# First stage in a written order: filter products one or two tiles ahead, scale's last half between them

## The chip, the cores and the metric

The kernel runs on one core of a Trainium2 chip. The metric is the device time of one execution in microseconds (us). The engines are TensorE (PE; its weight loads are shown apart as PEld), VectorE (DVE), ScalarE (ACT), GpSimd (POOL), and SyncE (SP), which here only issues DMAs. PSUM is the memory that TensorE writes; a bank holds 128 x 512 fp32.

## The reference, cut to what matters

The model is three blocks in a row on an input of 512 tokens by 1024 channels: attention with dilations beside a gated recurrence, then a block with latent attention and a long convolution, then a hybrid block. The change lies in what is done before the first projection. Four pieces of it are computed there.

```
# block 1: modulated norm of the input
mod = silu(c) @ w_ada + b_ada;  shift, scale, gate = split(mod, 3)
h = rmsnorm(x, norm_g) * (1 + scale) + shift
q_a, k_a, v_a, ... = split(h @ w_in)
# block 1: table of relative biases for the attention (rel_bias, by bucket of distance)
# block 2, wanted much later: filters of the long convolution and an embedding
h = sin(fr * (z @ w1 + b1)); h = sin(fr * (h @ w2 + b2)); h = sin(fr * (h @ w3 + b3))
h = (h @ w_out).reshape(L, 2, 512) * decay       # forward and backward filter
kf = rfft(concat(h_fwd, 0, reversed h_bwd))      # spectrum of the filter
e = p @ w_ple                                    # per-layer embedding
```

## The kernel before, in words

All activations are held transposed: 8 tiles of 128 channels by 512 tokens. A product is made nearly exact in fp32 by splitting each operand into a high part (rounded, written by ACT) and a low part (the rest, a subtraction on DVE or POOL), and by three matmuls, high with high, low with high and high with low (`acc_T`). `parts` splits a weight tile of 128 x 1024, `split` an activation, into the tiles `wh` and `wl`, or a high and a low tile. Weights are loaded by SP into four raw buffers (`wr`) that are handed out in turn; there are three pairs of `wh` and `wl`.

The order of instructions on each engine is set by a planner, which keeps the order of the data and takes, at each moment of its own clock, the work that is ready, what was written earlier first. Where the kernel opens a region with `manual_schedule`, the instructions of the named engines keep the order in which they are written; how the engines stand against each other, and where work from outside the region falls between, stays with the planner. Before the change only TensorE's order in the recurrence of block 1 is written so. Each engine's queue is worked off in order: an instruction that waits holds everything behind it.

The stage is the function `start`. Its parts:

- `early.load0`, `load1`, `load_fw`: the loads for the work that block 2 needs (positions `c_z`, filter layers `fw`, embedding input `pt`, its weights `w2ple`, filter output weights `fwo`, decays `dec`, transform matrices `c_fw`).
- `early.layer(i)`: a product of 64 by 64 for both halves of the positions, a reduction of the angle on DVE (seven operations), and a sine on ACT; three in a row.
- `early.emb`: eight products of the embedding with 6 matmuls each, copied out of PSUM by ACT into the tiles A, which hold the normed input later, and stored to memory (`scr_e`).
- squares of the input x on ACT, their sum on DVE, `col_sums` (TensorE), `rsqrt` (a DVE operation and a power on POOL), `rows` (TensorE spreads the result over the partitions, ACT copies it to `bc`).
- `early.filt(t)`, for four tiles of time: two filter products into banks `s`, two products with the decay on DVE, their sum on POOL and difference on DVE, and the splits of both: `sm` with the low part on DVE, `df` with it on POOL.
- `AdaRows`, for scale and for shift: eight tiles `adar` of 512 KB, six buffers for both; four thin matmuls per tile (32 columns of weights, 256 elements moved), accumulated in the one bank `o`; then `columns`: a copy on ACT, two transposes, an addition on DVE.
- DVE multiplies each x tile with the gain and `bc`; with shift, ACT writes the high part of the tile A, DVE its low part. This is `h`.
- `early.spectrum(f)`, for two halves of the frequencies: 24 matmuls on `sm` and `df` (`halves`), ACT copies, POOL's difference and sum, stores to `scr_kf` that are issued from ACT's queue.
- `rel_table`: two products, copies to a tile, a store, from which the attention's loads are made.

Of the second spectrum and of the table, TensorE's part is put behind the transposes of shift (`issue_after`). The first projection, `attn1`, starts with the product of `w1q` with `h` in `proj_T`.

## Time and profile before

| | us |
|---|---|
| median of the timed runs (3; 2255.76 to 2261.93) | 2259.17 |
| the profiled execution: its own time | 2263.86 |
| its span | 2262.1 |
| TensorE busy in the span (97%) | 2193.2 |
| DVE busy (61%) | 1372.2 |
| ACT busy (42%) | 947.0 |
| POOL busy (23%) | 529.1 |
| first matmul of q's projection starts at | 84.75 |

The span is that of one profiled execution. A line of the profile names the line of the kernel, the engine, the operation, what it writes and what it reads; x is the count, and in brackets or behind a bar stands the idle time of the engine before it, with what ended it. A line of a helper (L116 is the matmul) stands for many places, so the names of the tiles tell which one is meant: `pa` is the embedding, `fwo` a filter product, `adar` a tile of scale or shift, `sm` and `df` the spectrum, `A` the normed input. An fp32 matmul appears as two instructions. The granted clock is TensorE's, as a share of full speed.

### The profile page before, as it was taken

What the parts mean: (1) busy time and instruction counts of PE and PEld (TensorE: products, weight loads), DVE (VectorE), ACT (ScalarE), POOL (GpSimd) and SP (SyncE); (2) the same over time, 40 slices, a digit from 0 to 9 for tenths busy, and PEclk for the clock granted to TensorE, in tenths of its full rate; (3) what the DMA queues carried; (4) which work ended last, traced back from release to release, by engine and by line L of the source; (5) the groups of instructions that cost most, each with busy time, mean ns of one, the idle gap of its engine ahead of it and who ended that gap; (6) DMA issues with size and microseconds to landing.
All of it is one profiled execution on the core that took longest, in us unless ns stands there. A gap on an engine that the chain in (4) does not pass through costs nothing.

```text
span 2262.1 us, 30194 instructions
## 1 busy us (share of the span) xinstructions
PE 2193.2 (97%) x11672; PEld 1793.4 (79%) x11672; DVE 1372.2 (61%) x2226; ACT 947.0 (42%) x1597; POOL 529.1 (23%) x454
## 2 busy tenths in 40 slices
PE   7898999999999998999999999999999999999998
PEld 4677788888888976688888886798888788888886
DVE  6564777753354598478647647877666754433333
ACT  4344556642243456544324434455544233222221
POOL 3233555521122225221001103000111221310220
PEclk7899999999999999999999999999999999999999
DMA  8552122224323342233232243222222422223322
GB/s 317 183 162 75 54 94 85 84 75 130 103 88 110 115 136 75 68 109 101 79 110 102 70 153 118 87 83 75 80 95 83 140 84 94 94 83 112 98 79 76
DMA packets 80728, 235.27 MB, mean 104 GB/s; under 512 B 9887, under 2 KB 10911, under 8 KB 80584
## 3 DMA queue, kind: packets, MB, share of 16 engines
q1 hardware_dynamic: 65768, 208.25, 28.2%
q10 hardware_dynamic: 14816, 25.08, 3.4%
q8 instruction: 92, 1.51, 0.3%
q14 instruction: 52, 0.43, 0.1%
HBM read 218.60 MB, written 15.22 MB: 103 GB/s over the span
## 4 chain that ended last, share of the span: by engine, by line
PE 56%; DVE 2%; issue 2%; ACT 1%; POOL 0%; POOLq 0%; DVEq 0%; ACTq 0%
PE mm L116 49%; PE s L116 3%; PE o L116 2%; PE t L116 1%; DVE sg L1772 0%; PE t L1612 0%; ACT wh L110 0%; DVE x L2438 0%; DVE st L1597 0%; DVE wl L111 0%; DVE x L1773 0%; DVE B L212 0%; PE t L2123 0%; ACT A L211 0%; PE t L2086 0%
## 5 line engine op out<-in xcount | busy, mean ns | idle before, releaser
L116 PE MATMUL mm<-A,wh 128*128 128x512 f32 x2176 | 691.1, 393 | 1.0 <-DVE A L212 1.0
L110 ACT CAST wh<-wr 128x1024 fp32r<-128x1024 f32 (+2 forms) x374 | 368.4, 987 | 609.6 <-PE mm L116 398.5
L111 DVE TENSOR_TENSOR wl<-wr,wh 128x1024 fp32r<-128x1024 f32 (+3 forms) x371 | 446.2, 1204 | 275.4 <-ACT wh L110 274.3
L116 PE MATMUL mm<-B,wh 128*128 128x512 f32 x1672 | 536.2, 396 | 1.3 <-DVE us L268 0.9
L116 PEld LDWEIGHTS mm<-A,wh 128*128 128x128 f32 x2176 | 409.6, 189 | 89.3 <-issue 1.9
L116 PE MATMUL mm<-A,wl 128*128 128x512 f32 x1088 | 425.8, 392 | 4.3 <-DVE wl L111 4.3
L116 PEld LDWEIGHTS mm<-B,wh 128*128 128x128 f32 x1672 | 313.5, 188 | 72.7 <-issue 4.0
L116 PE MATMUL mm<-B,wl 128*128 128x512 f32 x836 | 329.2, 394 | 0.0
L116 PEld LDWEIGHTS mm<-A,wl 128*128 128x128 f32 x1088 | 205.4, 189 | 47.7 <-DVE wl L111 6.3
L116 PEld LDWEIGHTS mm<-B,wl 128*128 128x128 f32 x836 | 157.3, 188 | 35.0 <-issue 3.0
L251 POOL TENSOR_TENSOR r<-r,mhalf 128x4 f32<-128x4 f32 (+1 forms) x40 | 53.2, 1332 | 407.6 <-DVE r L250 407.6
L116 PE MATMUL mm<-a,wh 128*128 128x512 f32 x448 | 140.5, 389 | 0.0
L268 DVE TENSOR_TENSOR us<-mm,bc 128x512 f32<-128x512 f32 x95 | 65.1, 688 | 97.2 <-PE mm L116 95.8
L204 POOL TENSOR_TENSOR a<-sl,a 128x512 fp32r<-128x512 f32 x28 | 40.5, 1446 | 274.2 <-ACT a L202 274.2
L116 PEld LDWEIGHTS mm<-a,wh 128*128 128x128 f32 x448 | 84.1, 188 | 17.5
L116 PE MATMUL mm<-a,wl 128*128 128x512 f32 x224 | 86.8, 389 | 0.0
L116 PE MATMUL mm<-wh,A 128*128 128x256 f32 x448 | 84.8, 285 | 0.0
L116 PEld LDWEIGHTS mm<-wh,A 128*128 128x128 f32 x448 | 71.0, 191 | 1.2 <-issue 0.6
L2358 POOL TENSOR_TENSOR sl<-sl,bc 128x512 f32<-128x512 f32 x22 | 28.7, 1305 | 167.6 <-DVE sl L1718 167.6
L116 PE MATMUL mm<-wl,A 128*128 128x256 f32 x224 | 63.6, 284 | 0.0
L116 PE MATMUL mm<-wh,B 128*128 128x256 f32 x320 | 61.2, 287 | 0.0
L1747 DVE TENSOR_TENSOR x<-x,mm 128x512 f32<-128x512 f32 x32 | 22.0, 687 | 64.5 <-PE mm L116 64.5
(588 smaller groups left out, 3472.0 us busy)
## 6 DMA issues: line engine op xcount, KB each, us to landing
wr<-w2upg SPq DMA_DIRECT2D x22, 512.0 KB, 3.4
wr<-w2upu SPq DMA_DIRECT2D x22, 512.0 KB, 3.4
wr<-w3fg SPq DMA_DIRECT2D x22, 512.0 KB, 3.4
wr<-w3fu SPq DMA_DIRECT2D x22, 512.0 KB, 3.4
adar<-w1ada SPq DMA_DIRECT2D x16, 512.0 KB, 7.6
wr<-w3out SPq DMA_DIRECT2D x16, 512.0 KB, 3.5
wr<-w1ib SPq DMA_DIRECT2D x14, 512.0 KB, 3.5
wr<-w2uh SPq DMA_DIRECT2D x12, 512.0 KB, 3.4
```

The lines of the kernel that those rows point to most:

```text
L110: nc.scalar.copy(out=hi[:, :n], in_=r[:, :n])
L111: (eng or nc.vector).tensor_tensor(out=lo[:, :n], in0=r[:, :n], in1=hi[:, :n].bitcast(F32), op=ALU.subtract)
L116: return self.nc.tensor.matmul(out, a, b, start=start, stop=stop)
L204: eng.tensor_tensor(out=l[:p], in0=src, in1=hi[:p].bitcast(F32), op=ALU.subtract)
L251: nc.gpsimd.tensor_tensor(out=r, in0=r, in1=self.mhalf[:, :n], op=ALU.pow)
L268: self.nc.vector.tensor_tensor(out=out, in0=ps, in1=bc, op=ALU.mult)
L1747: k.nc.vector.tensor_tensor(out=xs[n], in0=xs[n], in1=ps, op=ALU.add)
L2358: nc.gpsimd.tensor_tensor(out=s, in0=s, in1=norm.bc, op=ALU.mult)
```

## The change

All five engines' instructions in `start` now keep the written order, and that order is new.

- The loads: embedding inputs and weights alternate; the table's inputs come before x; then scale's first four tiles, filter output weights, decays, and shift's first four tiles. Scale has four buffers of its own; shift goes into the two tiles of each A(i), as halves of 256 KB. Scale's last four tiles, shift's others and the transform matrices follow. The embedding is held in eight tiles of its own and stored after all these loads; the spectrum's copies later use the same tiles.
- The embedding is issued in pairs, between the layers and scale's first half. Scale's first half comes before the filter, its second half after the rows of the norm, between the filter products.
- Filter products are issued one or two tiles before the work on their results, into banks `s` and `mm` by turns. Sum and difference are both on DVE, both low parts on POOL.
- The first transform matrix is split by POOL, the second by DVE. The spectrum is issued in four halves, one before shift's last tiles, one among the normed inputs, two at the end; its sums come last (the sum on DVE, the difference on POOL), and its stores go through SP.
- The load and the split of the first `w1q` tile are written in `start`, before the last two halves' products.

```diff
@@ proj_T
-            self.acc_T(ps, self.w(s, nk * P, eng), act, nk, i == 0, i == len(nks) - 1, k0=k0)
+            w, self.first = self.first or self.w(s, nk * P, eng), None
+            self.acc_T(ps, w, act, nk, i == 0, i == len(nks) - 1, k0=k0)
@@ AdaRows
-    def load(self):
+    def load(self, kks, places=None):
...
+        for kk in kks:
+            src = k.aps["w1ada"][self.part, kk]
+            if places:
+                r = places[kk]
+                for j in range(2):
+                    k.nc.sync.dma_start(out=r[j], in_=src[:, j * T : (j + 1) * T])
+            else:
+                t = self.pool.tile([P, D], F32, tag="adar", bufs=4, name=k.name("adar"))
+                k.nc.sync.dma_start(out=t, in_=src)
...
+    def step(self, n):
         k = self.k
-        ps = k.bank("o", 1)
-        for kk, r in enumerate(self.r):
+        if self.n == 0:
+            self.ps = k.bank(*(("mm", 3) if self.part == 0 else ("o", 1)))
+        for kk in range(self.n, self.n + n):
...
@@ start
-    with k.tc.tile_pool(name="b1s", bufs=1) as pool:
+    with k.tc.tile_pool(name="b1s", bufs=1) as pool, k.tc.manual_schedule(
+        engines={E.PE, E.Activation, E.DVE, E.Pool, E.SP}
+    ):
+        scale, shift = AdaRows(k, pool, 1), AdaRows(k, pool, 0)
         early.load0(pool)
+        rb, oh = rel_load(k, pool)
...
+        scale.load(range(4))
         early.load1()
...
+        places = [[t.bitcast(F32) for t in k.A(i)] for i in range(NK)]
+        shift.load(range(4), places)
...
+        early.layer(0)
+        early.parts(0)
+        early.sin()
+        early.parts(1)
+        early.emb(2)
+        early.layer(1)
+        early.emb(2)
+        early.sin()
+        early.layer(2)
+        square(2)
+        scale.step(2)
+        early.emb(2)
+        square(2)
+        early.sin()
+        scale.step(2)
+        scale.load(range(4, 8))
+        shift.load(range(4, 6), places)
+        early.load_fw(0)
+        shift.load(range(6, 8), places)
+        early.load_fw(1)
+        early.emb(2)
+        early.filt_ps(0)
+        square(4)
+        early.filt_ps(1)
+        sums = k.col_sums(acc)
+        early.filt(0)
+        r = k.rsqrt(sums, NT, 1.0 / D)
+        early.filt_ps(2)
+        shift.step(2)
+        bc = k.rows(r)
+        early.filt(1)
+        scale.step(4)
+        early.filt_ps(3)
+        early.store()
+        early.filt(2)
+        shift.step(2)
         sc1 = scale.columns()
+        early.fparts(0)
+        early.filt(3)
         (the gain of each x tile, then its product with the gain and bc, as before)
+        early.halves(0, 0)
+        shift.step(4)
         sh = shift.columns()
+        early.fparts(1)
+        tab = rel_table(k, rb, oh)
         (for each i: the high and the low part of A(i), as before)
+            if i == 4:
+                early.halves(0, 1)
+        k.first = k.w(k.aps["w1q"][0])
+        early.halves(1, 0)
+        early.halves(1, 1)
+        early.sums()
@@ Early2.filt_ps, filt
+            ps = k.bank(*(("mm", 3) if t % 2 else ("s", 2)))
+            k.mm(ps, self.cur[r, t % 2 * P : t % 2 * P + P], self.wo[r, j * 512 : (j + 1) * 512], True, True)
...
-            (nc.gpsimd if add else nc.vector).tensor_tensor(out=s, in0=fb[0], in1=fb[1], op=op)
-            l.append(k.split(k.pair(p, f"{nm}{t}"), s, lo="v" if add else "g"))
+            nc.vector.tensor_tensor(out=s, in0=fb[0], in1=fb[1], op=op)
+            l.append(k.split(k.pair(p, f"{nm}{t}"), s, lo="g"))
@@ Early2.fparts, halves, sums
+        self.fw_parts.append(self.k.parts(self.cw[f], eng=None if f else self.k.nc.gpsimd))
...
+                t = self.p.tile([P, T], F32, tag=f"e{4 * f + 2 * j + i}", name=k.name("ab"))
+                nc.scalar.copy(out=t, in_=ps)
...
             nc.gpsimd.tensor_tensor(out=d, in0=a, in1=b, op=ALU.subtract)
-            nc.gpsimd.tensor_tensor(out=a, in0=a, in1=b, op=ALU.add)
+            nc.vector.tensor_tensor(out=a, in0=a, in1=b, op=ALU.add)
             for i, s in enumerate((a, d)):
-                nc.scalar.dma_start(out=self.kf[j, 2 * f + i], in_=s)
+                nc.sync.dma_start(out=self.kf[j, 2 * f + i], in_=s)
```

More of the change, by code (lines that the diff above doesn't have):

```diff
@@ L495, in start @@
             xs.append(x)
+        scale.load(range(4))
         early.load1()
-        early.load_fw(0)
-        early.load_fw(1)
-        scale, shift = AdaRows(k, pool, 1), AdaRows(k, pool, 0)
-        scale.load()
+        places = [[t.bitcast(F32) for t in k.A(i)] for i in range(NK)]
+        shift.load(range(4), places)
         c = k.v("c", 0, 8)
@@ L506, in start, with square @@
         nc.vector.tensor_scalar(out=sc, in0=sc, scalar1=0.5, scalar2=None, op0=ALU.mult)
-        for i in range(3):
-            early.layer(i)
-        early.emb(range(NK))
         acc = k.nm.tile([P, T], F32, tag="sqa", bufs=1, name=k.name("xa"))
-        for i in range(NK):
-            q = pool.tile([P, T], F32, tag="xq", bufs=3, name=k.name("xq")) if i else acc
-            nc.scalar.activation(out=q, in_=xs[i], func=AF.Square)
-            if i:
-                nc.vector.tensor_tensor(out=acc, in0=acc, in1=q, op=ALU.add)
-        bc = k.rows(k.rsqrt(k.col_sums(acc), NT, 1.0 / D))
-        for t in range(NT):
-            early.filt(t)
-        shift.load()
+        qs = []
+        def square(n):
+            for i in range(len(qs), len(qs) + n):
+                q = pool.tile([P, T], F32, tag="xq", bufs=3, name=k.name("xq")) if i else acc
+                nc.scalar.activation(out=q, in_=xs[i], func=AF.Square)
+                qs.append(q)
+                if i:
+                    nc.vector.tensor_tensor(out=acc, in0=acc, in1=q, op=ALU.add)
+        early.layer(0)
[34 more added lines that the diff above has]
+        shift.step(2)
         sc1 = scale.columns()
+        early.fparts(0)
+        early.filt(3)
         ga = k.cp.tile([P, NK], F32, tag="gada", name="gada")
         nc.vector.scalar_tensor_tensor(out=ga, in0=sc1, scalar=1.0, in1=k.v("norm_g", 0, 8), op0=ALU.add, op1=ALU.mult)
-        early.spectrum(0)
         for i in range(NK):
@@ L537, in start @@
             h.append((hi, lo))
-        with k.tc.issue_after(mark):
-            early.spectrum(1)
-            tab = rel_table(k, pool)
+            if i == 4:
[4 more added lines that the diff above has]
+        early.sums()
     return h, tab
@@ L1221, in emb, with store, filt_ps @@
             k.acc_T(ps, (hi[:, o:], lo[:, o:]), self.pa, 2)
-            e = k.A(n)[0].bitcast(F32)
+            e = p.tile([P, T], F32, tag=f"e{n}", name=f"e{n}")
             nc.scalar.copy(out=e, in_=ps)
-            nc.sync.dma_start(out=self.ed[n], in_=e)
+            self.es.append(e)
+    def store(self):
+        for n, e in enumerate(self.es):
+            self.k.nc.sync.dma_start(out=self.ed[n], in_=e)
+    def filt_ps(self, t):
+        k = self.k
+        r = slice(t // 2 * 64, t // 2 * 64 + 64)
+        self.fps[t] = []
+        for j in range(2):
+            ps = k.bank(*(("mm", 3) if t % 2 else ("s", 2)))
+            k.mm(ps, self.cur[r, t % 2 * P : t % 2 * P + P], self.wo[r, j * 512 : (j + 1) * 512], True, True)
+            self.fps[t].append(ps)
+    fps = {}
     def filt(self, t):
@@ L1228, in filt @@
         fb = []
-        for j in range(2):
-            ps = k.bank("s", 2)
-            r = slice(t // 2 * 64, t // 2 * 64 + 64)
-            k.mm(ps, self.cur[r, t % 2 * P : t % 2 * P + P], self.wo[r, j * 512 : (j + 1) * 512], True, True)
+        for ps in self.fps[t]:
             f = self.tmp()
```

69 lines of the change are left out of this document (42 added, 27 removed).

## The prediction, as it stood before the result

> **What bounds the kernel now.** I read the page first (span, slices, granted clock), then the busy time by ten-microsecond stretch, TensorE in order of time, the groups by line, and the queue of SP.
>
> ```profile
> span 2262.1 us, 30194 instructions
> ...
> PEclk7899999999999999999999999999999999999999
> ```
>
> The granted clock is full in nearly all of the 40 slices, of 56.6 us each; the two first ones, where the change lies, are low. The profiled execution took 2263.86 us, 1.76 over its span and 4.69 over the median of the timed runs (2259.17).
>
> The stretches (PE, PEld, DVE, ACT, POOL busy; granted clock; DMA share; GB/s):
>
> ```profile
> 0.00:10.00 10.00, 1.11 (x4) 0.32 (x4) 4.89 (x10) 2.73 (x4) 3.85 (x11) 1.00 0.69 217
> 10.00:20.00 10.00, 8.64 (x30) 5.83 (x31) 7.50 (x14) 9.46 (x15) 0.00 (x0) 1.00 1.03 386
> 20.00:30.00 10.00, 8.85 (x60) 6.70 (x58) 7.36 (x13) 5.57 (x10) 3.69 (x2) 1.00 1.02 417
> 30.00:40.00 10.00, 9.35 (x40) 3.03 (x40) 4.67 (x8) 1.65 (x3) 4.43 (x4) 0.63 1.04 411
> 40.00:50.00 10.00, 10.00 (x17) 3.61 (x14) 6.90 (x7) 3.25 (x5) 4.56 (x4) 0.50 0.89 351
> 50.00:60.00 10.00, 9.17 (x36) 5.39 (x34) 4.51 (x5) 3.47 (x6) 4.64 (x4) 0.68 0.06 14
> 60.00:70.00 10.00, 4.96 (x50) 2.08 (x50) 7.26 (x11) 1.14 (x3) 4.87 (x4) 0.83 0.94 322
> 70.00:80.00 10.00, 6.95 (x29) 4.22 (x30) 3.74 (x7) 4.23 (x8) 0.00 (x0) 0.50 0.11 45
> 80.00:90.00 10.00, 10.00 (x43) 7.25 (x42) 4.64 (x7) 4.23 (x7) 5.99 (x4) 0.98 0.42 137
> ```
>
> DMA is full from 10 to 40 us and nearly so to 50, all but idle in 50:60 and busy again in 60:70. The reader is to see the second burst: late loads in a stage whose queues had room. TensorE in order of time:
>
> ```profile
> 11.29 1.65 PE L116 MATMUL mm<-pa,wh 128*128 128x512 f32 x3 [5.91 <-ACT wh L110]
> ...
> 26.80 1.05 PE L116 MATMUL t<-ident,r 128*128 128x128 f32 x8
> 27.78 1.07 PE L116 MATMUL o<-adar,silc 128*32 128x256 f32 x16
> 30.65 1.98 PE L116 MATMUL s<-fwo,fh 64*128 64x512 f32 x4 [1.80 <-ACT fh L1212]
> ...
> 34.43 3.78 PE L116 MATMUL s<-fwo,fh 64*128 64x512 f32 x4
> 38.14 1.93 PE L116 MATMUL o<-adar,silc 128*32 128x256 f32 x16
> ...
> 63.28 0.69 PE L476 MATMUL t<-ident,adarow 128*128 128x128 f32 x2 [4.11 <-ACT adarow L473]
> ...
> 72.49 2.23 PE L116 MATMUL o<-adar,silc 128*32 128x256 f32 x16 [4.09 <-DMA adar<-w1ada]
> ...
> 75.55 0.78 PE L116 MATMUL mm<-sm,wh 128*128 128x512 f32 x1
> ...
> 80.60 0.39 PE L116 MATMUL mm<-df,wh 128*128 128x512 f32 x1
> ...
> 82.08 1.24 PE L116 MATMUL t<-oh,rb 33*8 33x512 f32 x4
> ...
> 84.75 0.39 PE L116 MATMUL mm<-A,wh 128*128 128x512 f32 x1
> ...
> 95.66 0.28 PE L116 MATMUL mm<-wh,A 128*128 128x256 f32 x1
> ```
>
> The first product on the normed input starts at **84.75**; the q and k products end at 95.66, 48 instructions of 0.227 us, 5.5 us for each product of 24. So the stage's length is 84.75, and 2262.1 - 84.75 = 2177.35 us follow. Two things make it long: scale's transposes come only at 63.28, and shift's last loads, which wait for buffers that scale's reduction frees, hold TensorE until 72.49. The clock costs too: two filter products take 1.98 us at 30.65 and 3.78 at 34.43, the reduction of two ada tiles 1.07 and 1.93.
>
> **The change part by part.** Groups of that stage (count, busy us, mean ns of one):
>
> ```profile
> L111 DVE TENSOR_TENSOR wl<-wr,wh 128x1024 fp32r<-128x1024 f32 x7 | 9.1, 1299 | 11.1 <-ACT wh L110 11.1
> ...
> L1241 POOL TENSOR_TENSOR tmp<-tmp,tmp 128x512 f32<-128x512 f32 x4 | 7.0, 1762 | 6.8 <-DVE tmp L1234 6.7
> ...
> L1241 DVE TENSOR_TENSOR tmp<-tmp,tmp 128x512 f32<-128x512 f32 x4 | 6.0, 1493 | 0.6 <-POOL tmp L1237 0.6
> ...
> L1234 DVE TENSOR_TENSOR tmp<-s,dec 128x512 f32<-128x512 f32 x8 | 5.5, 690 | 9.5 <-PE s L116 8.5 <-issue 1.0
> L534 DVE SCALAR_TENSOR_TENSOR A<-x,adac,A 128x512 fp32r<-128x512 f32 x8 | 5.4, 749 | 0.8 <-ACT A L533 0.8
> L525 DVE SCALAR_TENSOR_TENSOR x<-x,gada,bc 128x512 f32<-128x512 f32 x8 | 5.4, 745 | 0.0
> L204 POOL TENSOR_TENSOR df<-tmp,df 128x512 fp32r<-128x512 f32 x4 | 5.1, 1274 | 3.8 <-ACT df L202 3.8
> ...
> L533 ACT ACTIVATE A<-x,adac 128x512 fp32r<-128x512 f32 x8 | 5.0, 710 | 1.0 <-DVE adac L478 1.0
> ...
> L515 DVE TENSOR_TENSOR xa<-xa,xq 128x512 f32<-128x512 f32 x7 | 4.8, 686 | 0.0
> ...
> L202 ACT CAST sm<-tmp 128x512 fp32r<-128x512 f32 x4 | 2.5, 616 | 5.4 <-POOL tmp L1241 5.4
> ...
> L251 POOL TENSOR_TENSOR r<-r,mhalf 128x4 f32<-128x4 f32 x1 | 1.0, 1022 | 14.2 <-DVE r L250 14.2
> ...
> L1237 POOL MEMSET tmp<- 1x512 f32 x1 | 0.5, 514 | 5.5 <-DVE tmp L1234 5.5
> ```
>
> No product is removed. I follow the written order to the first q product, at these prices. A DVE sum of two SBUF tiles is taken at 0.69 (a sum of squares, 686 ns); where POOL works at the same time it cost 1493, which is the upper bound.
>
> *To the filter.* The embedding starts at 11.3 as now. Before, its 48 products, with two layer products, the column sums and the broadcast rows, fill 11.29 to 27.78; half of scale's reduction (2 x 1.07) enters where sums and rows (about 1 each) leave. With some 0.4 for handovers TensorE reaches the first filter product at 28.3 instead of 30.65, the two prepared banks at 32.3. ACT must first copy the last embedding tile and square four x tiles, 0.6 each as a cast, and DVE adds the last: 28.3 + 3 + 0.7 = 32.0. Tile 0's four operations (2 x 0.69, a memset of row 0 of 0.51, 2 x 0.69) end at 35.2. The power for the norm now stands on POOL behind tile 0's two splits: a cast that starts 0.7 sooner, 0.62, then 2 x 1.27 and 1.02, 38.7. TensorE's rows wait for it, with scale's last half behind them.
>
> *Scale and filter 2, 3.* I keep the half clock from 33 on, since the same thin products ran at it. Two filter banks 3.8 (to 37), two ada tiles of shift 1.9 (38.9), rows 2.1 (41), four tiles of scale 3.9 (44.9), filter tile 3 3.8 (48.7), shift's second two 1.9 (50.6), transposes 0.7, DVE's column add: **51.6**. DVE waits there, while POOL splits the first spectrum weights unhurried (2.4, at twice DVE's 1.2), and tile 3, the gains and all of x are queued behind that one instruction. In return scale ends 12 us before its present place (transposes at 63.28).
>
> *Normed x and shift.* Tile 3's four DVE operations end at 54.4, its cast and POOL split at 56.3; the first spectrum half, whose first bank ran meanwhile, ends at 57.2; shift's last four tiles 3.9, row copy, transposes and column add with their handovers 1.4 by estimate (the transposes alone 0.69): **62.5**. DVE's eight x products need 54.4 + 5.4, plus up to 2.5 if they wait for POOL's two splits (bounds 59.8 and 62.3): hidden behind shift, and 2.5 more if TensorE came sooner. The shift loads no longer wait for other buffers: they go in 16 pieces of 256 KB into the later A tiles. Their bytes with all before them, 14.7 MB, need some 43 us by 10.2 MB up to 30 us (the stretches' GB/s) and 411 after. Two banks of TensorE work lie after that, so the move itself costs nothing; were that cover gone, shift's last tiles would wait, 0.6 us a piece.
>
> *The end.* DVE: weight split 1.2, table copies 1, eight lows 5.4, to 70.1; then q's weight, 1.2, 71.3, about 1.2 more since ACT's last three highs (0.6 each of the eight's 5.0) are queued behind the copies of the second half. TensorE: table 1.3; the first twelve spectrum products 5.1 (68.9), which is what twelve took from 75.55 to 80.60 before the clock was back; 24 more at 0.227, 5.5: **74.4**. TensorE is last. The eight kf stores move from ACT's queue to SP's, the embedding's behind the loads; nobody in the stage waits for either, so I take that as nought, and price the other bound as a rival.
>
> Sum: 84.75 - 74.4 = 10.4 us saved. 2263.86 - 10.4 = 2253.5 for an execution like the profiled one, 4.69 less for the median: **2249**. The own range is 2244 to 2254 (5 us each way: the 2.5 us of POOL, the memset, and the place of the clock's fall).
>
> A rule speaks against the clock that I kept. The Trainium skill, page "TensorE: Matmul & The Clock Gate", section "Part 1: The HAM clock gate", says that about 3.4 us of sustained activity gives full clock and an idle window takes it away. This trace differs: 0.50 in all of 40:50, with TensorE busy 10.00 of 10. By the rule the sum would be the second case below; by the row it is the one above.
>
> **The rivals.** *Full clock throughout.* The clock never falls between 28.3 and 57, the stage being tighter. For it: 20:30 at 1.00. Against it: 30:50, where the same filter and ada products stand at 0.63 and 0.50. Then DVE and POOL set the time: x products done near 60, lows at 67.6, q's split 68.8, q product at 69.2: 15.55 saved, 2243.6.
>
> *The next weights behind the stores.* Only the order on one engine is written; where other instructions fall between is left to the planner, so the change need not do all that it says. SP before:
>
> ```profile
> 25.42 0.33 SPq L97 DMA_DIRECT2D wr<-w1q  x1
> ...
> 27.97 0.33 SPq L97 DMA_DIRECT2D wr<-w1k  x1
> ```
>
> Time to landing (KB each, us):
>
> ```profile
> wr<-w1q SPq DMA_DIRECT2D x3, 512.0 KB, 8.0
> wr<-w1k SPq DMA_DIRECT2D x3, 512.0 KB, 4.5
> ```
>
> Four raw buffers are handed out in turn, and q's load is now written behind the table's store. If k's load also falls behind the eight kf stores, it issues after the last spectrum copy, difference and sum: 74.4 + 0.6 + 1.3 + 0.7 + 0.5 = 77.5, lands 4.5 to 8.0 later, and needs some 2.3 of casting (cast and split, 1.2 each at most): 84.3 to 87.8 against q's end at 79.9. 4.4 to 7.9 of the 10.4 go: 2253 to 2257, 2255. Against it: both loads stood before waiting stores in the old queue.
>
> *The half clock comes early* (slower than before). The written order breaks the embedding into pairs between layer products and tiles of scale. If those gaps drop the clock at 18 instead of 33, the place is TensorE up to the column sums: 24 products at +0.2 (5.05 / 12 against 0.227), two pairs of filter banks at +1.8, four tiles of scale at +1.7, the sums at about +1, 11.1 in all; and if it doesn't come back in the last 24 products, 4.8 more: 15.9 lost against 10.4 saved, 2264.5. It decides from 10.4 us of such loss on. For it: 40:50 shows that being busy isn't enough. Against it: 10:20 and 20:30 stand at 1.00, with layer products and ada tiles between the embedding's.
>
> **How the numbers follow.** Chances: forecast 0.50, full clock 0.18, loads behind stores 0.18, early half clock 0.14. 0.3% is 6.8 us, about what a measurement of this kernel tells from none; so faster means below 2252.4. Faster: 0.50 x 0.83 + 0.18 + 0.02 of the loads = 0.61; slower (above 2266): 0.10, half of the early half clock and 0.03 for a worse re-planning of what follows; the same: the remaining 0.29. The range of 2240 to 2263 leaves out a tenth above and less below.
>
> **What would show it.** Right: first filter product near 28, scale's column add near 52, shift's near 62, first product on A near 74, and no second burst of DMA before it. The clock in 33 to 60 separates the first two cases; the issue of k's load against the kf stores, and an idle TensorE after the q product, the third; the clock in 18 to 33 the fourth. I am wrong if the first product on A comes after 80, or if the part behind it, 2177.35 us now, changes by more than 3.

## The result, and the profile after

| | before | after | ratio, 95% interval |
|---|---|---|---|
| timed with the prediction, median | 2257.47 | 2245.58 (2243.64 to 2248.54, 4 runs) | 0.9946, 0.9929 to 0.9963 |
| timed again, beside e9, median | 2260.43 (9 runs) | 2247.63 (2246.61 to 2249.40, 5 runs) | 0.9950, 0.9936 to 0.9963 |

The changed kernel is about 12 us faster: 2245.58 against the forecast of 2249.0, inside its own range of 2244 to 2254. Its profiled execution took 2248.54, 1.84 over its span. First the page of the kernel after, span and granted clock:

```profile
span 2246.7 us, 30202 instructions
...
PEclk8999999999999999999999999999999999999999
```

The ten-microsecond stretches of the kernel after, in the columns of the prediction (PE, PEld, DVE, ACT, POOL; granted clock; DMA share; GB/s):

```profile
20.00:30.00 10.00, 9.01 (x63) 5.58 (x62) 5.28 (x12) 5.05 (x10) 0.00 (x0) 1.00 1.05 405
30.00:40.00 10.00, 9.31 (x26) 4.29 (x28) 7.61 (x13) 3.89 (x7) 2.77 (x3) 0.74 1.03 409
40.00:50.00 10.00, 9.58 (x60) 4.52 (x60) 3.78 (x5) 3.98 (x7) 6.65 (x6) 0.58 0.76 294
50.00:60.00 10.00, 8.23 (x67) 4.02 (x66) 8.36 (x10) 3.61 (x6) 7.46 (x5) 1.00 0.01 2
60.00:70.00 10.00, 6.96 (x19) 5.19 (x20) 8.40 (x14) 4.67 (x8) 0.18 (x1) 0.66 0.37 125
```

The second burst of transfers is gone: DMA is full until about 47 us and idle in 50:60. What moves after that, from 66 to 74 us, is the table and the attention's weights, and TensorE waits for none of it before the first product on A. DVE, at 4.51 in 50:60 before, is now busier there than TensorE (8.36 against 8.23). TensorE of the kernel after, in order of time (start, length, what ended an idle time ahead of it):

```profile
30.18 1.98 PE L116 MATMUL s<-fwo,fh 64*128 64x512 f32 x4
...
34.57 1.68 PE L116 MATMUL t<-ones,xa 128*128 128x1 f32 x8 [0.69 <-DVE xa L544]
36.18 3.78 PE L116 MATMUL s<-fwo,fh 64*128 64x512 f32 x4
39.88 1.93 PE L116 MATMUL mm<-A,silc 128*32 128x256 f32 x16
42.23 2.08 PE L116 MATMUL t<-ident,r 128*128 128x128 f32 x8 [0.42 <-POOL r L254]
44.24 3.64 PE L116 MATMUL o<-adar,silc 128*32 128x256 f32 x32
47.81 2.28 PE L116 MATMUL mm<-fwo,fh 64*128 64x512 f32 x4
...
51.02 0.44 PE L498 MATMUL t<-ident,adarow 128*128 128x128 f32 x2
...
56.17 1.93 PE L116 MATMUL mm<-A,silc 128*32 128x256 f32 x32
58.60 0.44 PE L498 MATMUL t<-ident,adarow 128*128 128x128 f32 x2 [0.49 <-ACT adarow L495]
...
63.05 0.59 PE L116 MATMUL t<-oh,rb 33*8 33x128 f32 x2 [3.06 <-DVE adac L500]
63.57 0.80 PE L116 MATMUL mm<-df,wh 128*128 128x512 f32 x1
...
74.49 0.39 PE L116 MATMUL mm<-A,wh 128*128 128x512 f32 x1
```

Shift's loads (now `A` with `silc`) hold nobody: the 4.09 us wait of before is gone. Shift's transposes are done at 59.0, but after two products of the table TensorE stands for 3.06 us, until DVE has done shift's column addition. Why, shows on DVE and on POOL of the kernel after:

```profile
51.50 0.17 DVE L500 TENSOR_TENSOR adac<-t,vec 128x8 f32<-128x8 f32 x1 [7.68 <-PE t L498]
...
54.38 8.54 DVE L588 SCALAR_TENSOR_TENSOR x<-x,gada,bc 128x512 f32<-128x512 f32 x8
62.84 0.15 DVE L500 TENSOR_TENSOR adac<-t,vec 128x8 f32<-128x8 f32 x1
```

```profile
54.40 1.30 POOL L207 TENSOR_TENSOR sm<-tmp,sm 128x512 fp32r<-128x512 f32 x1 [1.59 <-ACT sm L205]
55.65 1.73 POOL L207 TENSOR_TENSOR df<-tmp,df 128x512 fp32r<-128x512 f32 x1
57.34 1.72 POOL L1354 TENSOR_TENSOR tmp<-ab,ab 128x512 f32<-128x512 f32 x1
```

The eight x products (each x tile times the gain and `bc`) took 8.54 us, where before they took 5.39 with POOL idle. POOL works beside them: tile 3's two splits, and the difference of the first spectrum half. Shift's addition is queued on DVE behind them.

Three marks serve to compare the kernels below: the start of the first product on the normed input (74.49), the issue of the last store of the filter's spectrum to `scr_kf` (81.59 in the kernel after), and the last output of the first attention, `oa`, by the last start in its group. This group before and after:

```profile
L204 DVE TENSOR_TENSOR oa<-of,oa x4: 667/690/693, 160.1 to 237.3; 128x512 fp32r<-128x512 f32 x4
```

```profile
L207 DVE TENSOR_TENSOR oa<-of,oa x4: 670/684/1009, 146.7 to 222.5; 128x512 fp32r<-128x512 f32 x4
```

So 10.3 us are won at the first product and 14.8 at the last `oa`: the attention, whose code the change leaves alone, became 4.5 us shorter. From there to the last product on `oa` it took 377.4 before and 377.5 after.

| kernel | first product on A | last `scr_kf` store | last `oa` | `oa` less store | time, us (runs) |
|---|---|---|---|---|---|
| before | 84.75 | 89.2 | 237.3 | 148.1 | see above |
| after | 74.49 | 81.6 | 222.5 | 140.9 | see above |
| e1, no written order | 66.24 | 74.7 | 225.3 | 150.6 | 2248.54 (5) |
| e2, early loads alone | 71.30 | 79.9 | 230.5 | 150.6 | 2253.67 (10) |
| e3, filter products not ahead | 77.84 | 85.3 | 225.9 | 140.6 | 2249.70 (1) |
| e4, scale's half after the filter | 72.91 | 80.5 | 222.2 | 141.7 | 2246.32 (1) |
| e5, before again | 83.35 | 88.1 | 236.8 | 148.7 | 2258.47 (1) |
| e6, table last | 74.54 | 79.0 | 227.9 | 148.9 | 2251.99 (1) |
| e7, x products without POOL | 73.75 | 83.2 | 225.3 | 142.1 | 2249.19 (1) |
| e8, another order | 69.27 | 77.6 | 219.4 | 141.8 | 2246.10 (5) |
| e9, e8 with scale's columns sooner | 69.19 | 77.2 | 219.3 | 142.1 | 2244.80 (5) |
| e10, after again | 71.94 | 79.5 | 221.7 | 142.2 | 2247.63 (5) |
| e11, filter's sum on POOL | 77.54 | 85.5 | 227.4 | 141.9 | 2251.27 (1) |
| e12, k's load behind the stores | 74.89 | 80.7 | 236.3 | 155.6 | 2261.25 (1) |

The runs were taken on several chips, on which the median of the kernel before was 2255.48 to 2260.43, so the times of different lines can be compared to some 2 us only; the ratios below go by the kernel before on the same chip. Two executions of one kernel differ by up to 2.6 us at the first mark and by 0.8 at the last. The fifth column falls into groups, 140.6 to 142.2 and 148.1 or more; e6 shows what parts them.

### The profile page after: what moved, and what is told of

Its sections match the earlier page's. It is cut to its first block, busy times and chain, and to the rows that moved or that the text cites. A ratio compares the mean times of both kernels' runs of the same rounds, so it can differ in the third digit from the quotient of the medians.

```text
span 2246.7 us, 30202 instructions
## 1 busy us (share of the span) xinstructions
PE 2185.9 (97%) x11672; PEld 1793.0 (80%) x11672; DVE 1373.8 (61%) x2230; ACT 946.9 (42%) x1597; POOL 523.6 (23%) x450
## 4 chain that ended last, share of the span: by engine, by line
PE 57%; DVE 2%; issue 2%; ACT 1%; POOL 0%; POOLq 0%; DVEq 0%; ACTq 0%
PE mm L116 50%; PE s L116 3%; PE o L116 2%; PE t L116 1%; DVE sg L1873 0%; PE t L1713 0%; ACT wh L110 0%; DVE x L2539 0%; DVE st L1698 0%; DVE wl L111 0%; DVE x L1874 0%; DVE B L215 0%; PE t L2224 0%; ACT A L214 0%; PE t L2187 0%
## 5 line engine op out<-in xcount | busy, mean ns | idle before, releaser
L116 PEld LDWEIGHTS mm<-B,wl 128*128 128x128 f32 x836 | 157.3, 188 | 35.2 <-issue 2.8
```

The costliest lines, as they stand in the source:

```text
L116: return self.nc.tensor.matmul(out, a, b, start=start, stop=stop)
```

## The experiments

**e1: without the written order.** All of the change stays but the order on the engines, which is the planner's again.

```diff
-    with k.tc.tile_pool(name="b1s", bufs=1) as pool, k.tc.manual_schedule(
-        engines={E.PE, E.Activation, E.DVE, E.Pool, E.SP}
-    ):
+    with k.tc.tile_pool(name="b1s", bufs=1) as pool:
```

> The changed kernel without the region of written order: same loads, buffers and engines, but the planner orders the stage. If the written order makes the gain, the first product on A falls back to 79 to 85 us (74.49 in the changed kernel, 84.75 before) and the time to within 4 us of before. If the loads and buffers make it (shift into the A tiles, scale in four buffers, embedding in its own tiles), it stays at 72 to 77 and the time within 3 us of the changed kernel.

Measured: 2248.54 (2247.30 to 2249.72), ratio to before 0.9958, 0.9940 to 0.9976, which overlaps that of the changed kernel. The last `oa` comes at 225.3, 11.4 us or more before that of the kernel before (236.8 and 237.3) and about 3 after the changed kernel's. So most of the gain needs no written order. Its first product on A comes 5.7 us before that of e10 and its last store 4.8 us before, so at the end of the stage the written order is a loss; e1 loses this again in the attention (150.6 in the fifth column), and e6 shows by what. The clock was granted in full in all of 30 to 60 here, and that alone did not make the kernel faster.

**e2: shift's loads early, and nothing else.** In the kernel before, shift's tiles are loaded right behind scale's into the A tiles, and scale keeps four buffers; the embedding gets tiles of its own, and scale's accumulation a bank of its own.

```diff
@@ start, of the kernel before
         scale.load()
+        shift.load([[t.bitcast(F32) for t in k.A(i)] for i in range(NK)])
...
-        shift.load()
@@ columns
-        ps = k.bank("o", 1)
+        ps = k.bank("o", 1) if self.part else k.bank()
@@ emb
-            e = k.A(n)[0].bitcast(F32)
+            e = p.tile([P, T], F32, tag=f"e{n}", name=f"e{n}")
```

> The kernel before with one part of the change: shift's loads are issued right behind scale's, in halves, into the A tiles, scale keeps four buffers, the embedding has its own tiles; the planner orders all. Theory of the loads: the second burst of DMA and the 4.1 us wait for it vanish, first product on A at 75 to 79, time 6 to 10 us under before. Theory of the order: scale's transposes still come near 63, first product on A after 81, time less than 4 us under before.

Measured: 2253.67 (2251.20 to 2258.81, 10 runs), ratio 0.9985, 0.9973 to 0.9996; first product on A at 71.30, as early as in the changed kernel and earlier than either theory had it, but the last `oa` at 230.5, under half of the gain. By the ratio the time is less than 4 us under before, as the second theory had it. ACT of e2 (ACTq is its queue of DMA issues), and TensorE of e2:

```profile
55.87 4.04 ACTq L1264 DMA_DIRECT2D scr_kf<-tmp  x4
59.95 1.99 ACT L110 CAST wh<-wr 128x1024 fp32r<-128x1024 f32 x2 [4.55 <-POOL tmp L1262]
61.85 0.36 ACT L481 COPY adarow<-o 128x256 f32<-128x256 f32 x1
```

```profile
57.95 1.91 PE L116 MATMUL o<-adar,silc 128*32 128x256 f32 x32
62.26 0.71 PE L484 MATMUL t<-ident,adarow 128*128 128x128 f32 x4 [2.40 <-ACT adarow L481]
```

Both reductions are done at 59.9, and the columns still come at 62.26: ACT, which must copy them, is held by the stores of the spectrum in its own queue, which wait for POOL's sums, and then by two weight casts that stood behind the stores. The kernel before had the same; its copy came late for POOL's sum, and TensorE waited 4.11 us for it at 63.28:

```profile
62.85 0.37 ACT L473 COPY adarow<-o 128x256 f32<-128x256 f32 x1 [2.09 <-POOL tmp L1254]
```

That is the second thing which the change takes away, by issuing these stores from SP and by doing the sums last. e1 has it, e2 has not, and e1's last `oa` is 5.1 us earlier; but e1 has the other parts of the change too, so what the stores' move brings by itself was not measured. Later e2 pays again: at 85.00 DVE has waited 6.31 us for the last store of the spectrum before it can write a small tile (`lb`) of the next stage, ACT waits 9.25 us for that tile, and TensorE waits 4.72 us at 88.53 for a weight cast that stands behind it on ACT.

**e3: filter products not ahead.** The written order stays; each tile's filter products are written behind the work on the tile before, not ahead of it.

```diff
         early.filt_ps(0)
         square(4)
-        early.filt_ps(1)
         sums = k.col_sums(acc)
         early.filt(0)
         r = k.rsqrt(sums, NT, 1.0 / D)
-        early.filt_ps(2)
+        early.filt_ps(1)
         shift.step(2)
         bc = k.rows(r)
         early.filt(1)
+        early.filt_ps(2)
         scale.step(4)
-        early.filt_ps(3)
         early.store()
         early.filt(2)
+        early.filt_ps(3)
         shift.step(2)
```

> The changed kernel with each filter product issued just before the work on its result, one tile of look-ahead less. If look-ahead hides TensorE's turn, DVE waits for two banks at half clock three times, and the first product on A comes 3 to 6 us later, 77.5 to 80.5. If DVE and POOL or the wait for scale's transposes set the pace, it moves by less than 1.5 us.

Measured: first product on A at 77.84, last `oa` at 225.9, 3.4 to 4.2 us later than the changed kernel's two executions; time 2249.70 in one run. By this run, products ahead into several banks are worth 3 to 4 us at the last `oa`.

**e4: scale's last half after the filter.** Scale's tiles and columns are issued when all four filter tiles are done.

```diff
         early.filt(1)
-        scale.step(4)
         early.filt_ps(3)
         early.store()
         early.filt(2)
+        early.filt(3)
         shift.step(2)
+        scale.step(4)
         sc1 = scale.columns()
         early.fparts(0)
-        early.filt(3)
```

> The changed kernel with scale's last half behind all filter products and behind the work on filter tile 3 on DVE. If scale's place between the products carries gain, the x products start 3 us or more later and the first product on A comes at 77 or later. If the wait of DVE for scale (7.7 us before its column add at 51.5) is mere waste, tile 3 fills it and the first product on A stays at 74.5 or comes up to 3 us sooner.

Measured: scale's addition on DVE at 51.84 (51.50 in the kernel after), first product on A at 72.91, last `oa` at 222.2, time 2246.32: no loss. So scale's place between the filter products brought nothing: in the kernel after DVE waits 7.68 us for it with the ready work on tile 3 behind, and here DVE does that work first. TensorE of e4:

```profile
55.36 0.50 PE L116 MATMUL mm<-sm,wl 128*128 128x512 f32 x1 [2.55 <-POOL wl L111]
```

The wait has moved: TensorE now stands for the low half of the spectrum's weights, which POOL splits after tile 3 and beside the x products (7.43 us here).

**e5: the kernel before again**, with no edit, as a measure of the spread.

> The kernel before once more, for a second profile: its profiled execution (2263.86) stood 6 us over the median of its timed runs. If the profile is typical of the kernel, the first product on A comes within 1 us of 84.75 and the last part of the attention's output (oa) is written within 1.5 us of 237.3. If that execution lost time in the stage or in the attention, one of the two comes 3 us or more sooner here.

Measured: 2258.47, span 2256.7; first product on A 1.4 us sooner, last `oa` 0.5. From the last `oa` to the last product on `oa` it took 374.8, where the profile of before shows 377.4. In the twelve profiles of the other kernels this stretch took 374.7 to 375.0 or 376.4 to 377.7, whatever had been changed.

**e6: the table of biases last.** The two small products, the copies and the store that the attention's bias loads need come after the spectrum, about where the kernel before had them.

```diff
-        tab = rel_table(k, rb, oh)
         h = []
...
         early.sums()
+        tab = rel_table(k, rb, oh)
```

> The changed kernel with the table of biases at the very end of the stage, behind the spectrum. Theory: the attention gained (first product on A to last oa 148.0 us, 152.6 before) because the table is stored at 65 us, ahead of the first product on A, in place of behind it; then that stretch goes back to 151 us or more, while the first product on A comes up to 1 us sooner. If the gain has another cause, the stretch stays at 147 to 149.

Measured: first product on A at 74.54 and last store at 79.0, no later than in the kernel after, but the last `oa` at 227.9, 5.4 us later; 2251.99 in one run. The fifth column is at 148.9, where the kernel before has 148.1 and 148.7. On SP's queue, the kernel after (in e6 the table's store goes at 79.50):

```profile
65.06 0.28 SPq L414 DMA_DIRECT2D scr_tab<-oh  x1
...
65.78 0.43 SPq L97 DMA_DIRECT2D wr<-w1k  x1
...
81.59 0.47 SPq L1357 DMA_DIRECT2D scr_kf<-tmp  x1
```

The first copy of q on ACT, and the first product of scores on TensorE, of the kernel after:

```profile
87.38 0.59 ACT L634 ACTIVATE q<-mm 64x512 fp32r<-64x512 f32 x1 [0.61 <-DMA scr_kf<-tmp]
```

```profile
91.40 0.36 PE L116 MATMUL s<-k,q 128*128 128x256 f32 x1
```

And of e6:

```profile
84.49 0.59 ACT L634 ACTIVATE q<-mm 64x512 fp32r<-64x512 f32 x1 [3.12 <-DMA scr_kf<-tmp]
```

```profile
97.07 0.28 PE L116 MATMUL s<-k,q 128*128 128x256 f32 x1
```

Two things are to be seen. First, ACT's first write of the attention waits for the last store to `scr_kf` to land: in ten of the fourteen profiles it comes 5.4 to 6.2 us behind the issue of this store. The profile names the store as what ended the wait in both executions of before, in after, e1, e6, e8 and e12; in six others it names a load or a split, and in e2 ACT has no wait just there. By the code the attention's tiles are made after the stage's tiles are given up, and the stored ones are the last to come free; that this is the reason is read from the code and these waits, and no run tried it alone. Second, the first scores follow this copy of q by 4.0 us in the kernel after, by 12.6 in e6 and by 13.7 before: with the table early, the planner puts the first scores between the two halves of v's product, and in e6 and before behind both. TensorE isn't idle there in either, so no wait shows it; what is late without the early table are the softmax and all that hangs on it, and at the end of the attention TensorE waits 6.9 us for `p` in e6, 4.0 after. The place of the scores is what parts the groups of the fifth column: they stand between the halves of v in all eight profiles of the lower group, and behind both in all six of the upper. In e1 and e12 they stand behind, 11.3 us after the first copy in e1, though the table's store is as early (66.84 and 65.48): it is the planner's choice, and the table only one of the things that set it.

**e7: the x products without POOL beside them.** Tile 3's low parts and the first spectrum difference go from POOL to DVE, so that POOL is idle while DVE multiplies x.

```diff
-            l.append(k.split(k.pair(p, f"{nm}{t}"), s, lo="g"))
+            l.append(k.split(k.pair(p, f"{nm}{t}"), s, lo="v" if t == 3 else "g"))
...
-            nc.gpsimd.tensor_tensor(out=d, in0=a, in1=b, op=ALU.subtract)
+            (nc.gpsimd if f + j else nc.vector).tensor_tensor(out=d, in0=a, in1=b, op=ALU.subtract)
```

> The changed kernel with POOL's work beside the x products taken to DVE: both low parts of filter tile 3 and the difference of the first spectrum quarter. If DVE's eight x products (8.54 us, 5.39 before) wait for POOL, they take 5.4 to 6 and start 1.4 us later; shift's column add comes at 60.5 to 62 instead of 62.84, the first product on A at 72 to 74. If they are slow for another cause, they stay above 8 and the first product on A comes at 75.5 to 76.5.

Measured, on VectorE of e7:

```profile
56.75 5.39 DVE L588 SCALAR_TENSOR_TENSOR x<-x,gada,bc 128x512 f32<-128x512 f32 x8
62.05 0.16 DVE L500 TENSOR_TENSOR adac<-t,vec 128x8 f32<-128x8 f32 x1
```

The products are back at 5.39: POOL's work is what stretches them. But the end hardly moves (62.05 against 62.84), since DVE now does the splits itself and waits 0.69 us for each cast: the products start 2.37 later. First product on A at 73.75, between the two executions of the kernel after. The last `oa` is later, at 225.3, and this follows the last store: DVE, busy in all of 70 to 80, does its sums later, the store goes at 83.2, and TensorE stands for 2.83 us ahead of the first scores at 93.41. In the lower group it is the one case whose first mark comes before the kernel after's and whose store comes behind, and the end of the attention went with the store.

**e8: another order.** All squares before the last embedding pair, so that the sums come right after the first filter product; the power ahead of tile 0; scale's last half and columns last.

```diff
-        square(2)
+        square(4)
...
-        square(2)
+        square(4)
...
         early.filt_ps(0)
-        square(4)
-        early.filt_ps(1)
         sums = k.col_sums(acc)
-        early.filt(0)
         r = k.rsqrt(sums, NT, 1.0 / D)
+        early.filt_ps(1)
+        early.filt(0)
         early.filt_ps(2)
-        shift.step(2)
         bc = k.rows(r)
         early.filt(1)
-        scale.step(4)
         early.filt_ps(3)
+        shift.step(2)
+        early.filt(2)
+        scale.step(4)
         early.store()
-        early.filt(2)
         shift.step(2)
+        early.filt(3)
         sc1 = scale.columns()
         early.fparts(0)
-        early.filt(3)
```

> The changed kernel in another order: squares of x in fours behind layer 2, the power for the norm on POOL ahead of filter tile 0's splits, filter tile 3 issued before shift's and scale's tiles, its work on DVE ahead of scale's column add. If DVE's 7.7 us wait and the queueing behind POOL's splits are what the stage still loses, the x products end at 56 to 59 (62.9 in the changed kernel) and the first product on A comes at 68 to 71; the time 3 to 6 us under the changed kernel. If TensorE's half clock sets the pace all the same, it stays within 2 us of 74.5.

Measured: first product on A at 69.27, last `oa` at 219.4, 2.3 to 3.1 us before the kernel after. 2246.10 (2242.73 to 2247.90), ratio 0.9957, 0.9943 to 0.9970: in time no difference from the kernel after can be told, and the 3 to 6 us that were expected did not show. VectorE and TensorE of e8:

```profile
48.95 7.42 DVE L587 SCALAR_TENSOR_TENSOR x<-x,gada,bc 128x512 f32<-128x512 f32 x8
```

```profile
47.52 0.69 PE L498 MATMUL t<-ident,adarow 128*128 128x128 f32 x2 [4.02 <-ACT adarow L495]
...
51.24 0.80 PE L116 MATMUL mm<-sm,wl 128*128 128x512 f32 x1 [1.99 <-POOL wl L111]
```

The x products start 5.4 us sooner, since DVE works through all four filter tiles before it needs scale and then waits 1.71 us for it, not 7.68. The clock helps here too: it was back at about 36.6, some twelve microseconds sooner than in the kernel after. TensorE now waits, 4.02 and 1.99.

**e9: e8 with scale's columns sooner**, ahead of the fourth filter tile, and the first spectrum weights split on DVE.

```diff
-        early.filt(3)
         sc1 = scale.columns()
+        early.filt(3)
         early.fparts(0)
...
-        self.fw_parts.append(self.k.parts(self.cw[f], eng=None if f else self.k.nc.gpsimd))
+        self.fw_parts.append(self.k.parts(self.cw[f], eng=None))
```

> As e8, with scale's columns ahead of the fourth filter tile on ScalarE and VectorE, and the first spectrum weights split on VectorE instead of GpSimd. Theory (each engine's written order, with the prices of e8's rows): TensorE's idle 4.0 us ahead of scale's transposes and 2.0 us ahead of the second spectrum product of e8 go or shrink; VectorE's x products end at 55.5 to 57 instead of 56.4, so the end of x, and not of the fourth filter tile, stays what shift's column add waits for; shift's columns at 57 to 59 (59.53 in e8), first product on A at 66.5 to 69 (69.27), last output of the first attention at 217 to 219.5 (219.4); in time 2 us or less better than e8, so 2242 to 2246, and 0.993 to 0.996 of before. Rival (the x products cost the same wherever they stand and the rest of the chain is given): first product on A within 0.5 of 69.27.

Measured, on TensorE and on VectorE of e9:

```profile
48.84 0.80 PE L116 MATMUL mm<-sm,wh 128*128 128x512 f32 x1 [4.38 <-ACT wh L110]
```

```profile
51.00 5.39 DVE L587 SCALAR_TENSOR_TENSOR x<-x,gada,bc 128x512 f32<-128x512 f32 x8
59.19 0.17 DVE L500 TENSOR_TENSOR adac<-t,vec 128x8 f32<-128x8 f32 x1 [2.79 <-PE t L498]
```

The x products end at 56.4, as expected. But shift's addition comes at 59.19 and the first product on A at 69.19, within 0.1 of e8: the theory missed here, and the rival's number stands, for another cause than it named. DVE is no longer last; it waits 2.79 us for TensorE, whose 4.02 us of waiting have only moved behind the transposes (4.38, for the cast of the spectrum's weights, which ACT has behind tile 3's). Time 2244.80 (2240.89 to 2248.04), ratio 0.9934, 0.9919 to 0.9948. Beside it on the same chip the changed kernel took 2247.63; four of e9's five runs are below the lowest of the changed kernel's five, one is above their median. That is 2.8 us by the medians, with overlapping intervals: probably a little faster than the changed kernel, not surely.

**e10: the changed kernel again**, with no edit.

> The changed kernel as it is, beside e9 and the kernel before on one chip. Theory: 2243 to 2249, ratio 0.993 to 0.997; first product on A 74.0 to 75.0, clock back between 47 and 51, last attention output 222 to 223.5; the stretch behind it takes one of the two values seen in all runs (374.8 or 377.5). If the clock's return were luck of one execution: half clock to 60 and first product on A at 76.5 to 78.

Measured: 2247.63; first product on A at 71.94, 2.1 us before the range expected for it, last `oa` at 221.7, a little before. The clock was back earlier than in the first execution, and earlier than expected. Two-microsecond stretches of the kernel after, and of e10:

```profile
40.00:42.00 2.00, 1.81 (x16) 0.47 (x16) 2.00 (x3) 0.00 (x0) 2.00 (x2) 0.50 1.05 417
...
46.00:48.00 2.00, 2.00 (x21) 0.73 (x14) 0.00 (x0) 1.05 (x3) 2.00 (x3) 0.50 0.62 237
48.00:50.00 2.00, 2.00 (x4) 0.69 (x4) 0.00 (x0) 1.26 (x2) 2.00 (x3) 0.89 0.02 6
```

```profile
44.00:46.00 2.00, 2.00 (x28) 0.92 (x20) 0.00 (x0) 1.88 (x4) 1.59 (x2) 0.57 1.06 408
46.00:48.00 2.00, 2.00 (x12) 0.67 (x4) 0.00 (x0) 1.32 (x2) 2.00 (x2) 1.00 0.72 276
```

**e11: the filter's sum on POOL again**, and the low part of the sum on DVE, as in the kernel before.

```diff
-            nc.vector.tensor_tensor(out=s, in0=fb[0], in1=fb[1], op=op)
-            l.append(k.split(k.pair(p, f"{nm}{t}"), s, lo="g"))
+            (nc.gpsimd if add else nc.vector).tensor_tensor(out=s, in0=fb[0], in1=fb[1], op=op)
+            l.append(k.split(k.pair(p, f"{nm}{t}"), s, lo="v" if add else "g"))
```

> The changed kernel with the filter's sum back on GpSimd and the low half of that sum back on VectorE, as before: the part 'splits on the vector engine' undone. Theory (VectorE's operations of two SBUF tiles take longer exactly where GpSimd works, so it is the total of both that counts): a tile's chain changes by under 1 us, first filter tile done 0.5 to 1 later, first product on A within 1.5 of 74.5, time within 2 us of after. Rival (the move of the sum to VectorE is what shortens the filter): each tile 1 to 1.5 us longer, first product on A 77 to 80.

Measured: first product on A at 77.54, last `oa` at 227.4, 2251.27 in one run: the theory fell, the rival stands. VectorE of e11:

```profile
37.89 0.69 DVE L207 TENSOR_TENSOR sm<-tmp,sm 128x512 fp32r<-128x512 f32 x1 [2.60 <-ACT sm L205]
...
45.47 0.69 DVE L207 TENSOR_TENSOR sm<-tmp,sm 128x512 fp32r<-128x512 f32 x1 [5.02 <-ACT sm L205]
```

It isn't the total of both engines that counts but the way of the data. With the sum on POOL and its low part on DVE, each tile goes from DVE to POOL, to ACT and back to DVE, and DVE stands for the way back, 2.60 and 5.02 us in the first two tiles, with the next tile queued behind. With both on DVE and both low parts on POOL, nothing comes back to DVE.

**e12: k's load behind the stores**, the third case of the prediction made true.

```diff
@@ start
         early.sums()
+        k.mark = next(i for i in reversed(nc.cur_bb.bb.instructions) if i.engine == E.SP)
@@ proj, in attn1
+            if pr == 0:
+                with k.tc.issue_after(k.mark):
+                    k.first = k.w(k.aps["w1k"][0])
             ps = k.proj_T([k.aps["w1k"][pr]], h)
```

> The changed kernel with the load of the first k weights held behind the last store of the filter's spectrum, as the third case of the prediction had it. By that case: load issued at 81 to 83 instead of 65.8, TensorE idle 4.4 to 7.9 us ahead of the k product, last attention output 4 to 8 us later, time 2250 to 2254. Rival (other work of TensorE, the v product or the second q product, fills the gap): last attention output under 2 us later.

Measured, on SP's queue and on TensorE of e12:

```profile
81.33 0.63 SPq L97 DMA_DIRECT2D wr<-w1k  x1
```

```profile
88.02 0.80 PE L116 MATMUL mm<-A,wh 128*128 128x512 f32 x1 [7.48 <-ACT wh L110]
```

TensorE's wait is as the prediction had priced it (4.4 to 7.9); the issue came 3.8 us later than its 77.5. The price of the whole is larger: the last `oa` comes at 236.3, 13.8 us after the kernel after's, and the time is 2261.25, no better than before. The first scores come at 107.9 instead of 91.4, since the planner has put them behind both halves of v's product. In e6, where they stand as late and k's load is early, the fifth column is 148.9; here it is 155.6, 6.7 more, which is near TensorE's wait. So about half of the price is the wait, and the other half the planner's order, which the prediction had not counted.

## Why the prediction was right, step by step

**The sum came out: 74.4 was forecast for the first product on A, 74.49 and 71.94 were seen.** But the agreement to 0.1 us is luck: it rests on two errors of like size, and a third lies ahead of them. What held is the path: shift's loads without a wait, scale's addition 12 us sooner, shift's addition and then TensorE's own products last.

*To the filter: 1.9 late.* The first filter product was forecast for 28.3 and came at 30.18, hardly before the old 30.65. Tile 0 was done at 37.6 on DVE, not 35.2; POOL's power at 42.2, not 38.7, behind tile 0's splits as said. Scale's addition still came at 51.50, where 51.6 was forecast, because of the next point. (The loads: by the rates that the prediction cites their bytes need until 41 us, not 43; nothing hangs on it, since TensorE has no wait for a load of shift.)

*The clock: failed at "I keep the half clock from 33 on".* It fell near 35, but was back at about 48.4, and at about 45.7 in the second execution (worked out from 0.89 of full speed in 48:50 and 0.57 in 44:46, as steps between 0.50 and 1.00). So the fourth filter tile took 2.28 us instead of 3.8, two tiles of shift 1.07 instead of 1.9, and shift's last four 1.93 instead of 3.9: 4.3 us less on TensorE, which had shift's transposes done at 59.0. It fell again in the 3.06 us wait (0.55 in 62:63), and the first twelve products of the rest took 5.28, as forecast (5.1).

*The x products: failed at "hidden behind shift".* The price with POOL beside it was in the text, at up to 2.5 us for two splits. It was 3.15 (8.54 - 5.39), since the first spectrum difference falls there too, which wasn't counted. More important, the products were not hidden: with TensorE 3.5 us sooner, shift's addition stood behind them until 62.84. The prediction had named this ("2.5 more if TensorE came sooner"), but not as the likely case. Forecast for the addition: 62.5. What the clock gave, DVE's queue took.

e8 speaks for DVE's queue as the one that counts: with 1.71 us of DVE's wait for scale left, the x products end 6.5 us sooner and the first product on A comes at 69.27. It doesn't show it alone, since its clock was back sooner too; e4, whose clock was not (0.50 until about 48.9) and whose DVE waits 1.45 us, has its x products end 2.4 us sooner. And in e7 the price of POOL was not had back by moving the splits to DVE: the total stayed.

*The end: right.* The table, twelve products at half clock and 24 at full clock took from 63.05 to 74.49; TensorE is last, with no wait.

*The stores: failed at "nobody in the stage waits for either".* Nobody in this stage waits for the stored data, but two others wait for the stores. ACT's copies of scale and shift stood behind them in its queue (e2); by this the forecast didn't lose, since it took scale's time from TensorE's order, but of the 12 us by which scale is sooner, which it put down to that order, 4.11 were this wait in the kernel before. And the first writes of the attention wait for the last store to land (rows at e6), so the attention's start seems to hang on this store, at 81.6, and not on the first product on A alone. In the eight profiles of the lower group the last `oa` follows the store by 140.6 to 142.2 us, and the first product on A by 148.0 to 151.5. It was not tried what an earlier store alone would bring.

*The rest: failed at "2177.35 us follow".* By span and first product 2172.2 us follow now, 5.1 less, over the 3 that the prediction had set itself. The term is the place of the first scores, between the halves of v's product, which e6 undoes by the table's place: 5.4 us at the last `oa`, over a third of the whole gain. The prediction gave the table 1.3 us of TensorE and did not ask what the planner would make of it in the attention. This is why the profiled execution took 2248.54 and not the 2253.5 of the sum; the forecast of 2249.0 lies 3.4 over the median.

**The rivals.** *Full clock throughout* (2243.6): the clock fell, so it isn't what happened; e1, with full clock in 30 to 60 but no order, took 2248.54. *Loads behind stores* (2255): k's load went at 65.78, ten microseconds before the first of the stores (75.87); e12 shows the mechanism real, its wait as priced (7.48), and the whole dearer (13.8 us at the last `oa`), since the planner then moved the scores too. *Early half clock* (2264.5): 20:30 stands at 1.00.

**Where the gain comes from**, at the last `oa` and by the nearest pairs: 6.6 us from shift's loads ahead of the need (e2), 5.1 from the other parts without the order, the stores off ACT's queue among them (e2 to e1), 3.2 from the written order (e1 to the mean of the two executions). The last is not won in the stage, where e1 has the first product on A and the last store sooner (66.24 and 74.7); it goes with the place of the scores. In the stage the order holds its own wait (DVE for scale, 7.68); e8 and e9, which shorten it, gain 2.3 to 3.2 us more at the last `oa`. Parts taken out one by one cost, at the last `oa`, 5.4 (e6, the table), 4.9 (e11, the sum on POOL), 3.4 (e3, products not ahead) and nothing (e4, scale's half), against the first execution of the kernel after; they aren't terms of a sum, since where one wait goes another can show.

## What to carry to other kernels

In a stage where four engines pass tiles on, look at each in-order queue for the one instruction that waits, and at what stands behind it: stores on an engine that computes, a reduction's last addition ahead of ready work, a sum that goes out and comes back. Price a moved step by who waits for its product or for its memory, in the next stage as well, and not by its own length. And when a term is a sum over engines, check which engine is last after every correction: an error of 4 us on TensorE was worth nothing once DVE had become last. Where a planner orders what follows, look at the order that it chose there as well: in e6 one small table, moved to the end of the stage, put the first scores 5.7 us later (97.07 against 91.40).

## What the runs showed of the hardware

*The clock differs between two executions of one kernel.* With the same instructions it came back at about 48.4 in one and 45.7 in the other, and the first product on A moved by 2.6 us, 1.1 of which was there at the first filter product already (30.18 and 29.07), with the clock still full. That the rest is the clock's alone isn't shown. The Trainium skill, page "TensorE: Matmul & The Clock Gate", section "Part 1: The HAM clock gate", says that the activity window runs freely and that the same kernel therefore varies from run to run; this agrees with the two executions. Its 3.4 us of sustained work don't cover all: in the kernel after TensorE worked from 36.18 to 41.8 without a gap and stayed at 0.50, and before from 40 to 50. In e9, on the other hand, it was back at about 36 in the middle of filter products. What kind of work brings it back isn't settled by these runs.

*VectorE beside GpSimd.* Eight products of two SBUF tiles took 5.39 us with POOL idle (before, e7, e9), 7.42 with 2.3 us of POOL work beside them (e8), and 8.54 with 4.75 (after): 2.0 and 3.2 us more. The page "SBUF — State Buffer" of the Trainium skill, section "SBUF: two separate sides", describes the port pair of the two engines as an exclusive lock held for a whole instruction, not a shared bandwidth; the first case agrees almost fully, the second with two thirds of POOL's time.

*Two lengths of one stretch.* From the last `oa` to the last product on it the trace shows 374.7 to 375.0 or 376.4 to 377.7 us, for the same kernel and whatever the change. One profile can therefore not tell a change of 3 us by its span; marks ahead of this stretch can.
